# A decoder step on one core: another order of the first loads, filler transposes at the start, another order of the attention jobs

## The chip, the core and the metric

The kernel runs on one core of a Trainium2 chip. Its engines are TensorE (PE, with its weight loads as PEld), VectorE (DVE), ScalarE (ACT), GpSimd (POOL) and SyncE (SP, which here only issues DMAs). The metric is the device time of one execution in microseconds, the median of several runs.

## The reference

One inference step of a two-layer decoder with conditioning, for a prompt of 512 tokens and eight samples of 8 tokens, model width 1024, everything in float32. Cut to its shape:

```python
def trunk(x, c, ...):                       # c: one conditioning vector for each sequence
    for l in range(2):
        sh1, sc1, g1, sh2, sc2, g2 = split(silu(c) @ ada_w[l] + ada_b[l], 6)
        h = rms_norm(x, norm_g[l, 0]) * (1 + sc1) + sh1
        if l == 0:
            # h @ w_in -> xr, yg; causal depthwise conv of width 4 on xr; RG-LRU:
            #   g = sigmoid(conv(xr) @ gate_w + gate_b) -> r, i
            #   log_a = 8 r log_sigmoid(rnn_lambda);  h_t = a h_{t-1} + sqrt(1 - a^2) i x_t
            out = (rg_lru(...) * gelu(yg)) @ rnn_w_out
        else:
            out = sliding_window_attention(rope(h @ w_q), k, v, sinks) @ attn_w_o
        x = x + g1 * out
        h = rms_norm(x, norm_g[l, 1]) * (1 + sc2) + sh2
        x = x + g2 * ((silu(h @ w_gate) * (h @ w_up)) @ ffn_w_out[l])
        if l == 0:
            k, v = ...                      # own conditioning, norm, projection, rope on k
    return rms_norm(x, final_g), new states and key/value windows
```

## The kernel before

The 576 tokens stand in two halves of 288 columns (256 of the prompt, 32 of the samples), A and B. The stream x is kept transposed: 8 chunks of 128 features on the partitions, 288 columns. A weight matrix is cut into *units* of 8 tiles of 128x128. A unit is loaded into one of 4 `raw` buffers (524 KB, one DMA), then split in `convert` into a high and a low part (`wh`, 10 buffers): a cast on ScalarE and a subtract on VectorE. Activations `h` are split likewise. `product` then makes 24 matmuls of 128x288 for a unit and a half: three for each of the 8 chunks of h.

Each function below doesn't issue its instructions. `Recorder.add` records them, with the tiles that they read and write and an estimated cost, and `schedule` then plays all engines forward in time and picks for each engine the recorded instruction with the best start time, weighted with its place in the record (`prio`; `early(n)` moves a block n places ahead). The five queues run in exactly the order that `schedule` finds; the chip has no part in the choice. VectorE and GpSimd share a port in this model (`port`). SP's issues may be taken up to 60 places (SPW) out of the recorded order. Buffers are handed out with a reserve for those recorded earlier. Since every instruction is emitted in one helper, all lines of the profile are L447, and the tile names tell the instructions apart: `reg` tiles hold x before it is transposed and conditioning weights, `sl` tiles small vectors and intermediates.

The record begins with the head. c (36 KB), the samples of x and x tiles 0 and 1 are loaded on SP, then two vector loads; nine small loads go out on GpSimd's queue, among them `rnn_lambda` as eight rows of a shared tile v2. `x_half(0)` squares and transposes the first x tiles. `ada_first_load(c)` loads the columns of the first shift and scale (SH1, SC1) for chunks c and c+1, 8 DMAs of 262 KB (2.1 MB), for c = 0, 2, 4, 6, the third into `reg` buffers, of which there are five, and the others into `wh`. `ada_first(c)` multiplies them by the conditioning: 32 products of 32x128 into one PSUM tile, each of them two instructions in the trace, so 64; the four groups make 256. `ada_turn` copies the result (ScalarE) and transposes it, `ada_end` adds bias and gain (VectorE), and `modulated` makes h for these two chunks and both halves. Weight units are loaded in between (`load_more`), one before each further group. `vectors_rest` transposes v2 and the states, and `decay_rates` computes the decay's constant from `rnn_lambda` with a chain of small operations of 128x8 on VectorE; the gates of the recurrent block need it. The units come in the order x0, x1, x2, the two gate units, x3 and so on (RNN, line 52).

After the head come the recurrent block (to about 170 us), the first feed-forward block, keys and values (from about 650 us), attention (to about 810 us), the second feed-forward block and the final norm. ATT (line 53) lists the attention stage: q is a query unit (24 matmuls for a half), a an attention chunk (scores, softmax on VectorE and ScalarE, values), s a sample, f the end of a half, o an output unit; A and B are the halves.

## Time and profile before

| | us |
|---|---|
| time, median of 3 runs (1274.91 to 1280.13) | 1275.53 |
| the profiled execution | 1275.33 |
| its span | 1273.5 |
| TensorE busy | 1246.1 |
| VectorE busy | 905.7 |
| ScalarE busy | 659.4 |
| GpSimd busy | 488.2 |

The span is the time from the first instruction to the last of the profiled execution; the rest of its time lies around it. Busy time of TensorE counts from a matmul's start to its modelled end, and matmuls are pipelined: a run of instructions that overlap is all busy, however densely they follow. [...]

### The profile page before, as it was taken

What the parts mean: (1) busy time and instruction counts of PE and PEld (TensorE: products, weight loads), DVE (VectorE), ACT (ScalarE), POOL (GpSimd) and SP (SyncE); (2) the same over time, 40 slices, a digit from 0 to 9 for tenths busy, and PEclk for the clock granted to TensorE, in tenths of its full rate; (3) what the DMA queues carried; (4) which work ended last, traced back from release to release, by engine and by line L of the source; (5) the groups of instructions that cost most, each with busy time, mean ns of one, the idle gap of its engine ahead of it and who ended that gap; (6) DMA issues with size and microseconds to landing.
All of it is one profiled execution on the core that took longest, in us unless ns stands there. A gap on an engine that the chain in (4) does not pass through costs nothing.

```text
span 1273.5 us, 25461 instructions
## 1 busy us (share of the span) xinstructions
PE 1246.1 (98%) x9568; PEld 1172.8 (92%) x9568; DVE 905.7 (71%) x2156; ACT 659.4 (52%) x1469; POOL 488.2 (38%) x709
## 2 busy tenths in 40 slices
PE   7999999999999999999999999999999999999997
PEld 5798899899998998999999997999999999999997
DVE  6988885775584686467578878558857758757856
ACT  4788873762352354145357768538424425524522
POOL 3476640131551552345024436110435345335511
PEclk8999999999999999999999999999999999999999
DMA  9956554416646556444432321322333323323232
GB/s 306 315 174 199 182 166 149 157 52 211 187 141 178 180 160 199 155 150 136 125 83 56 69 76 38 111 84 96 90 94 83 100 84 96 96 78 97 71 96 75
DMA packets 223981, 165.40 MB, mean 130 GB/s; under 512 B 23757, under 2 KB 209065, under 8 KB 223826
## 3 DMA queue, kind: packets, MB, share of 16 engines
q1 hardware_dynamic: 223410, 163.45, 42.5%
q8 instruction: 75, 1.23, 0.4%
q14 instruction: 48, 0.39, 0.1%
q0 software_dynamic: 448, 0.32, 0.1%
HBM read 160.85 MB, written 4.87 MB: 130 GB/s over the span
## 4 chain that ended last, share of the span: by engine, by line
PE 73%; DVE 13%; ACT 6%; POOL 4%; issue 2%; DMA 1%; SPq 0%; ACTq 0%; POOLq 0%; DVEq 0%
PE mm L447 69%; PE ada L447 4%; DVE wh L447 4%; DVE sl L447 4%; POOL raw L447 3%; ACT wh L447 2%; DVE ta L447 1%; DMA reg<-in_x_prompt_dram 1%; DVE td L447 1%; ACT tb L447 1%; ACT h L447 1%; ACT sl L447 1%; ACT ta L447 1%; DVE tb L447 1%; DVE h L447 1%
## 5 line engine op out<-in xcount | busy, mean ns | idle before, releaser
L447 PE MATMUL mm<-h,wh 128*128 128x288 f32 x4128 | 596.8, 299 | 3.5 <-ACT h L447 2.1
L447 PEld LDWEIGHTS mm<-h,wh 128*128 128x128 f32 x4128 | 562.4, 189 | 21.7 <-issue 9.9
L447 PE MATMUL mm<-sl,wh 128*128 128x288 f32 x3218 | 462.4, 296 | 0.8 <-ACT ta L447 0.8
L447 PEld LDWEIGHTS mm<-sl,wh 128*128 128x128 f32 x3218 | 436.9, 188 | 9.4 <-issue 5.9
L447 ACT CAST wh<-raw 128x512 fp32r<-128x512 f32 (+3 forms) x388 | 266.4, 710 | 292.4 <-PE mm L447 208.4
L447 DVE TENSOR_TENSOR wh<-raw,wh 128x512 fp32r<-128x512 f32 (+3 forms) x388 | 344.9, 913 | 60.1 <-ACT wh L447 54.0
L447 POOL TENSOR_TENSOR raw<-raw 128x512 f32<-128x512 f32 x76 | 109.8, 1445 | 183.9 <-DVE wh L447 154.1
L447 POOL TENSOR_TENSOR x<-x,ta 128x32 f32<-128x32 f32 x152 | 58.7, 386 | 306.8 <-DVE ta L447 306.7
L447 DVE SCALAR_TENSOR_TENSOR x<-mm,mods,x 128x256 f32<-128x256 f32 x160 | 77.3, 483 | 133.2 <-PE mm L447 132.1
L447 POOL TENSOR_TENSOR raw<-raw,raw 128x512 f32<-128x512 f32 x76 | 111.8, 1471 | 3.7
L447 PE MATMUL mm<-tb,wh 128*128 128x288 f32 (+1 forms) x488 | 89.7, 299 | 4.5 <-POOL sl L447 1.6
L447 PEld LDWEIGHTS mm<-tb,wh 128*128 128x128 f32 x488 | 72.3, 188 | 9.4 <-DVE td L447 5.4
L447 POOL TENSOR_TENSOR td<-td,td 128x288 f32<-128x288 f32 x38 | 32.0, 843 | 111.9 <-ACT td L447 106.5
L447 ACT ACTIVATE ta<-x 128x288 f32<-128x288 f32 x56 | 24.3, 443 | 67.2 <-POOL x L447 62.1
L447 PE MATMUL mm<-ta,wh 128*128 128x288 f32 (+1 forms) x254 | 55.9, 298 | 0.0
L447 DVE TENSOR_TENSOR td<-mm,td 128x288 f32<-128x288 f32 x76 | 33.2, 452 | 27.9 <-PE mm L447 27.9
L447 PE MATMUL ada<-reg,cz 128*32 128x512 f32 (+1 forms) x448 | 49.5, 553 | 0.0
L447 DVE TENSOR_TENSOR sl<-ta,sl 128x288 fp32r<-128x288 f32 x54 | 44.9, 834 | 1.7 <-ACT sl L447 1.5
L447 ACT COPY td<-mm 128x256 f32<-128x256 f32 (+1 forms) x102 | 34.2, 353 | 20.4 <-PE mm L447 18.4
L447 DVE TENSOR_TENSOR sl<-td,sl 128x288 fp32r<-128x288 f32 x50 | 38.2, 764 | 8.1 <-ACT sl L447 8.1
L447 ACT ACTIVATE ta<-mm 128x288 f32<-128x288 f32 x54 | 21.4, 410 | 43.2 <-PE mm L447 41.8
L447 PEld LDWEIGHTS mm<-ta,wh 128*128 128x128 f32 x254 | 41.5, 188 | 1.8 <-ACT wh L447 0.8
(202 smaller groups left out, 1248.4 us busy)
## 6 DMA issues: line engine op xcount, KB each, us to landing
raw<-in_ffn_w_in_dram SPq DMA_DIRECT2D x88, 512.0 KB
reg<-in_ada_w_dram SPq DMA_DIRECT2D x80, 512.0 KB
raw<-in_ffn_w_out_dram SPq DMA_DIRECT2D x32, 384.0 KB
raw<-in_ffn_w_out_dram SPq DMA_DIRECT2D x32, 320.0 KB
raw<-in_rnn_w_in_dram SPq DMA_DIRECT2D x16, 512.0 KB
reg<-in_kv_ada_w_dram SPq DMA_DIRECT2D x16, 512.0 KB
wh<-in_ada_w_dram SPq DMA_DIRECT2D x24, 256.0 KB
raw<-in_rnn_w_out_dram SPq DMA_DIRECT2D x8, 512.0 KB
```

Source lines behind the costliest of these rows:

```text
L447: self.rec.add(eng, lambda: getattr(obj, name)(*map(real, args), **{k: real(v) for k, v in kw.items()}), cost, outs, ins, func, lat, port, ...
```

## The change

The start of the record is written anew. `rnn_lambda` gets a load and a tile of its own, the first load on GpSimd's queue; `decay_rates` transposes it itself and stands near the start of the record, 200 places later in priority (DK). SP's loads up to weight unit 2 are recorded in one piece and issued in exactly that order (`strict`). `keep_busy(200)` records 200 transposes of the identity into a PSUM tile that nothing reads; `schedule` takes one on PE only where its next other instruction would start more than 250 ns (FILL) later, and drops those left over once all up to `idle_end` is done. `ada_first` puts its products into the queue in batches of 8 (first group) or 16 (the others), which nothing can come between, and its transpose goes to the conditioning's own PSUM pool. The order of attention jobs is another, the model's rule for the shared port is another, and conditioning products are planned at n/2.4 + 6 instead of n/2.4 + 30 ns. The arithmetic of the outputs stays the same.

```diff
-ATT = ("q0A q2A a0A q1A q0B a2A a1A q1B q3A a0B q2B a1B q4A a3A a4A q3B a2B q5A q4B a3B q6A a5A q5B q7A a6A a4B s0A "
-       "q6B a5B s1A s2A s3A q7B a7A s0B a6B fA s2B a7B s1B o0A s3B o1A fB o2A")
+ATT = "q0A q2A a0A q1A q0B a2A q1B q3A a0B q2B q4A a1A a1B a4A a3A q3B a2B q5A q4B a3B q6A a5A q5B q7A a6A a4B s0A q6B a5B s1A s2A s3A q7B a7A s0B fA s2B a6B a7B s1B o0A s3B o1A o2A fB"
...
+FILL = 250
+DK = 200
+AF_ = (1, 2, 2, 2)
...
                 for pr, i, op in avail[e]:
-                    if e == "SP" and i > sp_next + SPW:
+                    if op.idle:
+                        fill = fill or op
+                        continue
+                    if e == "SP" and i > sp_next + (SPW if i >= self.strict else 0):
                         break
...
                     if op.port == 1:
-                        s = max(s, port - 130 if e == "DVE" else port + 20)
+                        s = max(s, port - 100 + (60 if holder == e else 0))
...
+                if fill and fill.prio <= limit:
+                    at = alloc_time(fill, f)
+                    if at is not None:
+                        s = max(f, fill.ready, at)
+                        if pick is None or pick[1] > s + FILL:
+                            pick = (0, s, fill, False)
...
-                cost = n / 2.4 + 30 if dt == F32 else n / 9.6 + 15
+                cost = n / 2.4 + 6
...
+    lam_ = sl()
+    lam = lam_.f[0:8, 0:P]
+    G.dma_start(lam, a["rnn_lambda"][0].rearrange("(r p) -> r p", p=P))
...
     def decay_rates():
...
+        pt = aux()
+        T.transpose(pt[:, 0:8], lam, ident[0:8, 0:8])
+        V.tensor_copy(lamT, pt[:, 0:8])
...
-    def ada_first(c):
+    def ada_first(c, m):
         o = ps(pada, "ada")
-        for q, b in enumerate(first_w[c]):
-            for k in range(2):
-                ada_mm(o, 2 * q + k, [b.f[:, n : n + P] for n in (256 * k, 256 * k + P, 512 + 256 * k, 512 + 256 * k + P)], q + k == 0, q + k == 4)
-            b.done()
-        t = ada_turn(o, 1)[:, 0:P].rearrange("p (g c b) -> p g c b", g=2, c=2)
+        for q0 in range(0, 4, m):
+            with rec.together():
+                for q in range(q0, q0 + m):
+                    b = first_w[c][q]
+                    for k in range(2):
+                        ada_mm(o, 2 * q + k, [b.f[:, n : n + P] for n in (256 * k, 256 * k + P, 512 + 256 * k, 512 + 256 * k + P)], q + k == 0, q + k == 4)
+                    b.done()
+        t = ada_turn(o, 1, ps(pada, "ada"))[:, 0:P].rearrange("p (g c b) -> p g c b", g=2, c=2)
...
-    x_half(0)
-    ada_first_load(0, whs)
-    vectors()
-    load_more(1)
+    def keep_busy(n):
+        with rec.when_idle():
+            t = aux()
+            for i in range(n):
+                T.transpose(t[:, 0:P], ident[:], ident[:])
+
+
+    keep_busy(200)
+    with early(-DK):
+        decay_rates()
+    load_more(nload[0] - nconv[0] + 1)
     for t in (2, 3):
         x_load(t)
+    ada_first_load(0, whs)
+    convert()
+    load_more(nload[0] - nconv[0] + 1)
+    ada_first_load(2, whs)
+    ada_first_load(4, regs)
+    convert()
+    ada_first_load(6, whs)
+    load_more(nload[0] - nconv[0] + 1)
+    convert()
+    rec.strict = len(rec.ops)
+    x_half(0)
+    vectors()
     H[0], H[1] = hkind[0](F32R), hkind[1](F32R)
     for c in range(0, KC, 2):
-        if c < 6:
-            convert()
-        ada_first(c)
-        if c < 6:
-            load_more(ST[c // 2])
-            ada_first_load(c + 2, (whs, regs, whs)[c // 2])
+        ada_first(c, AF_[c // 2])
...
     vectors_rest()
+    rec.idle_end()
...
-    with early(100):
-        decay_rates()
```

## Rows read from the trace of the kernel before

**Rows 1.** The page's busy time, share of the span and instructions of each engine

```profile
PE 1246.1 (98%) x9568; PEld 1172.8 (92%) x9568; DVE 905.7 (71%) x2156; ACT 659.4 (52%) x1469; POOL 488.2 (38%) x709
```

**Rows 2.** Stretches: us, busy (instructions) of PE, PEld, DVE, ACT, POOL, PEclk, DMA, GB/s

```profile
0.00:53.10 53.10, 43.03 (x414) 31.32 (x414) 39.65 (x179) 28.85 (x64) 15.81 (x37) 0.90 1.05 320
...
53.10:150.00 96.90, 96.87 (x724) 86.78 (x725) 83.43 (x162) 85.29 (x170) 66.00 (x143) 1.00 0.58 187
...
150.00:170.00 20.00, 17.10 (x126) 14.94 (x125) 14.79 (x27) 15.09 (x27) 11.34 (x27) 1.00 0.55 178
...
690.00:700.00 10.00, 8.32 (x63) 7.83 (x62) 9.06 (x22) 8.34 (x21) 6.23 (x6) 1.00 0.25 55
```

**Rows 3.** The head in stretches of 10 us, columns as above

```profile
0.00:10.00 10.00, 4.96 (x32) 4.83 (x33) 1.75 (x8) 5.15 (x8) 6.12 (x20) 1.00 0.76 232
10.00:20.00 10.00, 6.61 (x83) 3.77 (x81) 8.77 (x37) 3.76 (x9) 2.50 (x6) 0.99 1.11 339
20.00:30.00 10.00, 9.74 (x60) 6.70 (x60) 8.50 (x32) 5.77 (x13) 2.46 (x5) 0.50 1.11 345
30.00:40.00 10.00, 8.83 (x119) 6.01 (x118) 8.82 (x41) 5.07 (x13) 3.08 (x4) 1.00 1.14 328
40.00:50.00 10.00, 9.98 (x104) 7.48 (x105) 9.15 (x54) 6.00 (x15) 1.65 (x2) 1.00 1.11 344
```

**Rows 4.** The chain that ended last: start us, length us, what

```profile
12.63 8.10 DMA reg<-in_x_prompt_dram
...
250.09 49.77 PE mm L447 x372
```

**Rows 5.** TensorE in order of time: start us, length us, what, count

```profile
7.09 1.75 PE L447 MATMUL mm<-ident,reg 128*128 128x128 f32 x7
...
9.49 0.72 PE L447 MATMUL mm<-ident,reg 128*128 128x128 f32 x5
...
20.87 1.94 PE L447 MATMUL mm<-ident,reg 128*128 128x128 f32 x8
...
33.55 0.65 PE L447 MATMUL ada<-reg,cz 128*32 128x128 f32 x16
...
38.88 0.63 PE L447 MATMUL ada<-reg,cz 128*32 128x128 f32 x12
...
42.90 0.40 PE L447 MATMUL mm<-h,wh 128*128 128x288 f32 x1
...
47.15 0.63 PE L447 MATMUL ada<-wh,cz 128*32 128x128 f32 x12
...
48.24 4.67 PE L447 MATMUL mm<-h,wh 128*128 128x288 f32 x32
```

**Rows 6.** Groups of TensorE up to 53.1 us: what, count, busy us, mean ns

```profile
L447 PE MATMUL mm<-h,wh 128*128 128x288 f32 x94 | 19.9, 341 | 1.4 <-ACT h L447 1.4
...
L447 PE MATMUL ada<-wh,cz 128*32 128x128 f32 x192 | 11.6, 307 | 0.9 <-DVE cz L447 0.4
...
L447 PE MATMUL ada<-reg,cz 128*32 128x128 f32 x64 | 3.4, 279 | 0.0
...
L447 PE MATMUL mm<-ident,reg 128*128 128x128 f32 x32 | 6.1, 362 | 1.9 <-DVE tb L447 1.7
```

**Rows 7.** SyncE's issues in order of time, columns as in rows 5

```profile
4.13 5.77 SPq L447 DMA_DIRECT2D wh<-in_ada_w_dram  x8
```

**Rows 8.** The chain that ended last, around 690 us

```profile
690.95 2.86 DVE wh L447 x2
...
695.03 1.05 ACT wh L447
```

**Rows 9.** Groups of VectorE from 14 to 51.3 us, columns as in rows 6

```profile
L447 DVE TENSOR_SCALAR sl<-sl 128x8 f32<-128x8 f32 x35 | 5.8, 165 | 0.3
...
L447 DVE SCALAR_TENSOR_TENSOR sl<-sl 128x8 f32<-128x8 f32 x27 | 4.8, 182 | 0.5
...
L447 DVE TENSOR_TENSOR sl<-sl 128x8 f32<-128x8 f32 x18 | 3.5, 195 | 0.4
```

More of the change, by code (lines that the diff above doesn't have):

```diff
@@ L85 @@
 class Op:
-    __slots__ = ("i", "prio", "eng", "emit", "cost", "func", "preds", "succ", "npred", "ready", "allocs", "start", "end", "done", "lat", "tiles", "port", "mode")
+    __slots__ = ("i", "prio", "eng", "emit", "cost", "func", "preds", "succ", "npred", "ready", "allocs", "start", "end", "done", "lat", "tiles", "port", "mode", "idle")
 class Ref:
@@ L139, in __init__ @@
         self.batch = None
+        self.fills = []
+        self.strict = 0
     @contextmanager
@@ L152, in together, with when_idle, idle_end @@
         self.add(b[0][0], emit, sum(x[2] for x in b), [y for x in b for y in x[3]], [y for x in b for y in x[4]], mode=self.mode)
+    @contextmanager
+    def when_idle(self):
+        self.fills.append([len(self.ops), None, True])
+        yield
+        self.fills[-1][1:] = len(self.ops), False
+    def idle_end(self):
+        self.fills[-1].append(len(self.ops))
     def tile(self, pool, kind, cap, reserve, shape, dt, name):
@@ L183, in add @@
         op.eng, op.emit, op.cost, op.func, op.lat = eng, emit, cost, func, lat
-        op.port, op.mode = port, mode
+        op.port, op.mode, op.idle = port, mode, bool(self.fills) and self.fills[-1][2]
         op.preds, op.succ, op.allocs, op.tiles = set(), [], [], set()
@@ L232, in schedule @@
         cold = 0.0
-        port, mode = 0.0, 0
+        port, holder, mode = 0.0, "", 0
         pos = {n: j for k in self.order for j, n in enumerate(self.order[k])}
@@ L274, in schedule @@
         sp = deque(o.i for o in self.ops if o.eng == "SP")
-        rest = deque(sorted(self.ops, key=lambda o: o.prio))
+        rest = deque(sorted((o for o in self.ops if not o.idle), key=lambda o: o.prio))
         done = set()
+        fills = deque(self.fills)
         while n_left:
             best = None
+            while fills and (not rest or rest[0].prio >= fills[0][3]):
+                for op in self.ops[fills[0][0] : fills[0][1]]:
+                    if op.i in done:
+                        continue
+                    done.add(op.i)
+                    n_left -= 1
+                    if op.npred == 0:
+                        avail["PE"].remove((op.prio, op.i, op))
+                    for n in op.tiles & last.keys():
+                        last[n] -= 1
+                        if last[n] == 0:
+                            if n in got:
+                                slots[self.kind_of[n]].append(rel_at[n] + 260)
+                            got.add(n)
+                fills.popleft()
+            if not n_left:
+                break
             while sp and sp[0] in done:
@@ L288, in schedule @@
                 seen = 0
+                fill = None
                 for pr, i, op in avail[e]:
-                    if e == "SP" and i > sp_next + SPW:
+                    if op.idle:
+                        fill = fill or op
+                        continue
+                    if e == "SP" and i > sp_next + (SPW if i >= self.strict else 0):
                         break
@@ L332, in schedule @@
             if op.port == 1:
-                port = s + cost
+                port, holder = s + cost, e
             elif op.port == 2 and s + 60 < port:
@@ L627, in vectors_rest @@
         pt = aux()
-        T.transpose(pt[:, 0:88], v2[0:88, :], ident[0:88, 0:88])
-        V.tensor_copy(abT[:, 96:112], pt[:, 72:88])
-        V.tensor_copy(vecT[:, 32:104], pt[:, 0:72])
+        T.transpose(pt[:, 0:80], v2[0:80, :], ident[0:80, 0:80])
+        V.tensor_copy(abT[:, 96:112], pt[:, 64:80])
+        V.tensor_copy(vecT[:, 32:96], pt[:, 0:64])
+        V.tensor_scalar(hgb[:], vecT[:, 80:96], 0.5, None, ALU.mult)
         pt = aux()
@@ L646, in decay_rates @@
         z, neg, msk, scl, p_, w_, w2, s_ = [tw.f[:, 8 * i : 8 * i + 8] for i in range(8)]
-        V.tensor_scalar(hgb[:], vecT[:, 80:96], 0.5, None, ALU.mult)
+        pt = aux()
+        T.transpose(pt[:, 0:8], lam, ident[0:8, 0:8])
+        V.tensor_copy(lamT, pt[:, 0:8])
+        lam_.done()
         V.tensor_scalar(neg, lamT, -1.0, None, ALU.mult)
@@ L691, in ada_mm, with ada_turn @@
             T.matmul(o[32 * j : 32 * j + 32, 0 : _free(w)], cz[:, k, :], w, start=first, stop=last)
-    def ada_turn(o, n):
-        t = aux()
+    def ada_turn(o, n, t):
         for i in range(0, n, 2):
@@ L764, in ada_step @@
             if k == KC - 1:
[L765 removed]
+                t = ada_turn(o, 4, aux()).rearrange("p (q g c b) -> p g c q b", q=4, g=2, c=2)
                 for i, g in enumerate(pairs[u // 16]):
```

4 lines of the change are left out of this document (1 added, 3 removed).

## The prediction, made before the changed kernel ran

> **What bounds the kernel now.** I read the busy times of the page first. TensorE is busy 98% of the span [rows 1], so only three things can shorten the kernel: less idle time on TensorE, less time at its low clock, and a denser queue. Then I cut the span into stages. From 53.1 to 150 us TensorE is idle for 0.03 us; up to 53.1 us it is idle for 10.1 us and the granted clock averages 0.90; 150 to 170 us loses 2.9 us and 690 to 700 us loses 1.7 us [rows 2]. The head is thus the place to look, and the diff works mostly there.
>
> In slices of 10 us the head shows its limit: from 10 us on the DMA engines are busy all the time and move 328 to 345 GB/s, while TensorE sits at the low clock from 20 to 30 us and VectorE is busy for 8.5 to 9.15 of every 10 us [rows 3]. Busy is not the same as useful, so I weigh the work. A long run of 128x288 products takes 49.77/372 = 0.134 us each [rows 4]. Sixteen conditioning products take 0.65 us, one alone lasts 0.279, so they follow each other after (0.65-0.28)/15 = 0.025 us; five transposes at 9.49 us take 0.72, so with a last one of the same length (0.72-0.28)/4 = 0.11 us each [rows 5, 6]. Up to 53.1 us the queue holds 94 products, 256 conditioning products and 64 transposes, of which the 32 of the prompt are the largest group [rows 6]: 94 x 0.134 + 256 x 0.025 + 64 x 0.11 = 12.6 + 6.4 + 7.0 = 26.0 us of work. So the head loses 27 us. After it the queue is dense: 32 products in 4.67 us [rows 5].
>
> **The change, part by part.** *The loads.* I count bytes in the order of the queue. The rows of GB/s add up to 2.3 MB at 10 us, 5.7 at 20, 9.2 at 30 and 12.4 at 40 [rows 3]. The last x tile stands at 5.3 MB in the old order (about 18.7 us) and its transfer is over at 12.63 + 8.10 = 20.7 us [rows 4], so a load is usable some 2 us after its bytes have had their turn. The old order puts the last conditioning load at 13.1 MB, behind one rnn_gate unit: turn at 42, usable at 44 us. The new order puts weight unit 0 and x tiles 2 and 3 ahead of the conditioning and lets nothing but unit 1 in between: the four groups of 2.1 MB end at 5.3, 7.9, 10.0 and 12.1 MB, usable at 20.7, 28.3, 34.5 and 40.9 us, and unit 2 at 12.6 MB, 42.5 us. The first group comes 4.5 us later than before, the last 3 us earlier. On SP the same issues are made in another order, eight of them in 5.77 us [rows 7] for bytes that need 6.2, so SP stays ahead; but the strict order means that a load whose buffer isn't free holds all behind it. The buffers in question are the five of x and conditioning (free once x is transposed, by about 20 us) and the weight buffers, free as the first two groups are consumed (by 30 us), each earlier than the turn of the load that waits for it. If one were late, it would cost its lateness, up to 2 us.
>
> *What TensorE can do with them.* From the last conditioning product of a group (38.88 + 0.63) to a 128x288 product on its output (42.90) it took 3.4 us [rows 5]; I use 4. So by the new landings: group by group 0.4 to 1 us of conditioning, then, 4 us later, 24 products on units 0 and 1 (3.2 us) for each pair of chunks; TensorE waits for data through all of it. The gate is at the end: unit 2 lands at 42.5, its cast on ScalarE takes 1.05 and its subtract on VectorE 2.86/2 = 1.4 [rows 8], with about 1 us of queueing: 46 us. By then six chunks of units 0 and 1 are done (72 products), the last two chunks come from 45 to 48, and from 46 on there is work without a break: 36 products on unit 2, 36 on the last chunks. The useful work at 46 us is 72 x 0.134 + 6.4 + 7.0 = 23.0 us, a loss of 23.0 us against 27.1 before: **4.1 us gained**. Bounds: 7 us if unit 2 doesn't gate (the last products of a group then end at 42 with the loss at some 20), 1 us if VectorE is as late as before (the old head's last conditioning products end at 47.15 + 0.63 = 47.8, 3.8 us behind the landing at 44 [rows 5]).
>
> *The decay rates.* Their three large groups are 80 operations on VectorE, 14.1 us in all, spread over 14 to 51 us [rows 9], a stretch in which it is 85 to 92% busy [rows 3]. Their own load lets them start near 7 us, where VectorE is nearly idle (1.75 of the first 10 us). By the share of the time, 14.1 x 21/37 = 8 us of VectorE's work leave the stretch from 30 to 51 us. It isn't a gain of its own; it is why I let the new head follow its landings more closely. The first conditioning in batches of 8 and 16 products does the same for TensorE's queue: in the old head a single 128x288 product stands between two groups of conditioning, as at 42.90, and lasts 0.40 us [rows 5] where one in a run costs 0.134. I cost both at nothing beside the 4.1.
>
> *The fillers.* Up to 200 transposes of the identity where the planner sees TensorE idle for over 0.25 us. They carry no work; they can raise the clock and they can stand in the way. [...] The fillers start near 1.6 us, once the identity is built; if they ran at the low level as long as the old head's transposes did, until about 6 us, they would take 0.21 instead of the 0.107 planned there, 2 us of lag. The planned idle up to 46 us is 46 - 23 - 2 = 21 us, less some 40 gaps under 0.25 us that stay: 100 to 150 fillers, not all 200. Since each gap leaves slack, the lag is gone by 20 us, when the first group lands. Cost 0, bounds 0 to 3 us. The clock from 20 to 30 us is full then, which in a stretch that waits for data is part of the 4.1.
>
> [...]
>
> *The attention order.* At 690 to 700 us TensorE is idle for 1.7 us while VectorE is busy for 9.06 of 10; the chain runs through two weight subtracts of VectorE (2.86 us) and a cast (1.05) [rows 2, 8]. The new order puts three query products ahead of two attention chunks, whose softmax steps are VectorE and ScalarE work, so the conversions come earlier. I take 1.0 of the 1.7; bounds -1.5 (the same stall at another place) and 1.7.
>
> *The planner's costs.* Port rule and cost of conditioning products change orders only. No row shows what another order is worth; the nearest, the 2.9 us of 150 to 170 us, bounds it to 2 us either way. I take 0.
>
> The sum goes against the profiled execution, 1275.33 us (span 1273.5 and 1.8 around it), which is 0.2 below the median of the three: 1275.3 - 4.1 - 1.0 = 1270.2, or 1270.4 on the median. I forecast **1270.3 us**.
>
> **The rivals.** *Faster still.* VectorE free of the decay rates converts unit 2 at once, TensorE is dense from 44 us (6 us gained), the stall at 690 us goes wholly (1.7) and the one at 150 us partly (1): 1275.3 - 8.7 = 1266.6. For it: the lag of 3.8 us behind the landing. Against: unit 2 is last in the queue. *Given back.* The recurrent stage after the head keeps ScalarE busy for 85 and VectorE for 83 of 97 us [rows 2]; if they set its pace, the 4 us come back as idle time at 150 to 170 us: 1274.5. Against: TensorE is idle for 0.03 us there. *Fillers in the way, slower or level.* If all 200 go out, the point at which 26 us of work are done lies at 1.6 + 2 + 200 x 0.11 + 26 + 4 (gaps) = 55.6 us against 53.1: 2.5 us lost, 1277. It decides from about 175 fillers. *Slower: the fillers don't raise the clock.* 130 of them then take 0.1 us more each, 13 us, and the work among them is slow too; a few microseconds of that are hidden in waits for data, so 8 to 12 us reach the end: 1284. [...] *The fillers or the loads don't go where they should* (the planner's data times are wrong, and TensorE waits at the low clock as before): the loads alone then give 2 to 3 us, 1273.
>
> **How the numbers follow.** Forecast 0.38; faster still 0.29; given back or misplaced (1273 to 1274.5) 0.20; fillers in the way 0.09; clock not raised 0.04. About 0.5% (6.4 us) is what a measurement of this kernel can tell from no change: faster means under 1269.2, slower over 1281.9. The rival below that and a third of the forecast's band (1267 to 1273) make faster 0.42; slower is the last rival and a little of the one before, 0.05; the rest, 0.53, is within. The range reaches from 1264.5 (head 7, attention 1.7, other orders 2) to 1277.
>
> **What would show it.** Right: the x tiles ahead of the conditioning on SP, the last conditioning products by 43 us, fillers from under 2 us, a granted clock of 1.00 from 10 us on, decay operations over by 25 us, and about 32 more products of 128x288 done at 53 us (126 instead of 94). Wrong: conditioning products that end after 46 us, unit 2 converted after 48, more than 175 fillers, a low clock after 10 us, or new idle time at 150 to 170 us.

## The result, and the profile after

The changed kernel takes **1262.64 us** (median of 4 runs, 1261.47 to 1262.99) against 1276.53 of the kernel before, run beside it: a ratio of 0.989 (0.987 to 0.992). Forecast were 1270.3 us, with 1264.5 as the lower end. So the time fell by 13.9 us where 5 were forecast, and lies 1.9 us below the range. The profiled execution's span is 1261.1 us against 1273.5, that is 12.4 less.

The page's busy time after the change, to be held against [rows 1]:

```profile
PE 1246.3 (99%) x9704; PEld 1182.5 (94%) x9704; DVE 883.6 (70%) x2157; ACT 650.3 (52%) x1464; POOL 494.2 (39%) x709
```

TensorE is busy for as long as before, and yet 12 us are gone. VectorE does one instruction more and is busy for 22 us less. That is the first sign that something other than the head changed. The four stretches of [rows 2], after (us, busy time and instructions of PE, PEld, DVE, ACT, POOL, PEclk (the granted clock of TensorE as a share of full speed), DMA share, GB/s):

```profile
0.00:53.10 53.10, 50.34 (x561) 44.15 (x562) 38.48 (x183) 29.33 (x67) 16.54 (x40) 1.00 1.03 312
53.10:150.00 96.90, 96.83 (x728) 86.79 (x727) 83.72 (x154) 79.02 (x161) 67.77 (x139) 1.00 0.60 192
150.00:170.00 20.00, 19.96 (x149) 19.68 (x148) 19.03 (x36) 17.32 (x34) 12.20 (x23) 1.00 0.51 170
690.00:700.00 10.00, 10.00 (x77) 10.00 (x76) 7.97 (x23) 2.89 (x6) 6.36 (x12) 1.00 0.72 133
```

The idle time of 150 to 170 us and of 690 to 700 us is gone. The head is now filled (with transposes) at a granted clock of 1.00; how much useful work it does is told by the count of 128x288 products up to 53.1 us, 105 instead of 94:

```profile
L489 PE MATMUL mm<-ident 128*128 128x128 f32 x135 | 20.1, 300 | 1.4 <-POOL tst L572 1.4
...
L489 PE MATMUL mm<-h,wh 128*128 128x288 f32 x105 | 17.3, 309 | 0.3 <-POOL h L489 0.3
```

**Where the time went.** All kernels here run the same 8088 products of 128x288 (96 of them are of 128x300; numbered in order of time), so the start of product n is a clock that runs on useful work. The table gives, for one profiled execution of each kernel, how much longer (+) or shorter (-) each stage is than in the kernel before, in us. Products 0 to 400 are the head, to 1000 the rest of the recurrent block, to 3700 the first feed-forward block, to 4200 its end and keys and values (591 to 666 us before), to 4600 the first queries (to 741), to 5000 the attention (to 838), to 8087 the second feed-forward block. The last column is the mean, in ns, of the 54 subtracts `sl<-ta,sl`, of which more below. Two executions of one kernel (after, after_beside) differ by up to 1.5 us in a stage.

| kernel | time, ratio to before | to 400 | 1000 | 3700 | 4200 | 4600 | 5000 | 8087 | sum | ns |
|---|---|---|---|---|---|---|---|---|---|---|
| before, length of the stage | 1276.5 | 100.5 | 92.8 | 398.2 | 74.7 | 74.5 | 97.7 | 426.1 | | 834 |
| after | 1262.6, 0.989 | -1.2 | -2.9 | -0.5 | -3.4 | -3.3 | +2.2 | -3.4 | -12.5 | 502 |
| after_beside | 1261.9, 0.989 | -2.3 | -2.9 | -0.5 | -3.1 | -1.8 | +2.2 | -4.3 | -12.7 | 501 |
| port_only | 1268.5, 0.995 | -0.5 | -2.3 | +0.8 | -3.7 | -2.4 | +4.9 | -4.1 | -7.3 | 490 |
| port_att | 1266.8, 0.993 | +5.2 | -1.2 | -0.8 | -3.4 | -2.8 | +2.4 | -3.5 | -4.1 | 493 |
| head_only | 1271.5, 0.997 | -0.7 | -2.5 | -0.1 | -0.2 | +0.8 | +0.2 | -0.7 | -3.2 | 854 |
| att_undone | 1266.1, 0.991 | -0.9 | -2.9 | -0.5 | -3.4 | -2.4 | +4.9 | -4.1 | -9.4 | 501 |
| pool_half | 1279.5, 1.002 | -0.8 | -2.2 | +0.6 | -2.9 | -0.4 | +13.9 | -3.9 | +4.3 | 493 |
| placebo1 | 1283.8, 1.006 | +3.7 | -1.9 | -0.5 | -1.0 | +0.6 | +6.4 | -1.2 | +6.2 | 922 |
| after_beta | 1265.5, 0.992 | -1.6 | -3.4 | -0.9 | -3.6 | -4.7 | +7.7 | -3.6 | -10.0 | 491 |

The sum after is -12.5 us, and the head is the smaller part of it in these executions. Columns 4200 and 8087 separate by the port rule: -2.9 to -4.3 in the seven executions that have it or half of it, -0.2 to -1.2 in the two that don't.

### The profile page after: what moved, and what is told of

It is laid out like the page before. It is cut to its first block, busy times and chain, and to the rows that moved or that the text cites. A ratio compares the mean times of both kernels' runs of the same rounds, so it can differ in the third digit from the quotient of the medians.

```text
span 1261.1 us, 25732 instructions
## 1 busy us (share of the span) xinstructions
PE 1246.3 (99%) x9704; PEld 1182.5 (94%) x9704; DVE 883.6 (70%) x2157; ACT 650.3 (52%) x1464; POOL 494.2 (39%) x709
## 4 chain that ended last, share of the span: by engine, by line
PE 88%; ACT 5%; DVE 3%; DMA 2%; POOL 1%; issue 1%; SPq 0%; ACTq 0%; DVEq 0%
PE mm L489 84%; PE ada L489 4%; DMA wh<-in_ada_w_dram 1%; ACT h L489 1%; ACT ta L489 1%; ACT tb L489 1%; DVE sl L489 1%; ACT sl L489 1%; DVE ta L489 1%; DMA raw<-in_rnn_w_in_dram 1%; DVE wh L489 1%; ACT wh L489 1%; SPq L489 0%; ACT td L489 0%; ACT L489 0%
## 5 line engine op out<-in xcount | busy, mean ns | idle before, releaser
L489 DVE TENSOR_TENSOR wh<-raw,wh 128x512 fp32r<-128x512 f32 (+3 forms) x388 | 340.5, 900 | 63.9 <-ACT wh L489 59.6
L489 ACT COPY td<-mm 128x256 f32<-128x256 f32 (+1 forms) x102 | 33.5, 357 | 13.9 <-PE mm L489 13.9
L489 ACT CAST sl<-ta 128x288 fp32r<-128x288 f32 x54 | 23.4, 433 | 31.8 <-DVE ta L489 29.4
L489 ACT ACTIVATE ta<-ta,stat 128x256 f32<-128x256 f32 (+2 forms) x72 | 32.5, 474 | 9.6 <-DVE stat L489 9.3
```

Of the source, the lines that this page charges most:

```text
L489: self.rec.add(eng, lambda: getattr(obj, name)(*map(real, args), **{k: real(v) for k, v in kw.items()}), cost, outs, ins, func, lat, port, ...
```

## The experiments

### The parts apart

port_only is the kernel before with the new port rule alone. In this rule `port` is the time at which the planner expects the port of its model, the one that it lets VectorE and GpSimd share, to be free, and `holder` the engine that took it last. The old rule lets VectorE start up to 130 ns before that time and GpSimd no sooner than 20 ns behind it; the new one lets either start 100 ns before it, or 40 if it is the holder itself. port_att has the new attention order and the new cost of conditioning products besides; head_only is the changed kernel with these three undone; no_fillers is the changed kernel without its transposes of the identity.

```diff
-        port, mode = 0.0, 0
+        port, holder, mode = 0.0, "", 0
...
-                        s = max(s, port - 130 if e == "DVE" else port + 20)
+                        s = max(s, port - 100 + (60 if holder == e else 0))
...
-                port = s + cost
+                port, holder = s + cost, e
```

> The kernel before with the planner's new rule for the port that VectorE and GpSimd share, and nothing else. Theory 1: the gain outside the head (11 of 12.4 us by the progress of the 128x288 products) comes from this rule, whose orders keep the two engines off each other: busy time of VectorE falls by about 15 to 22 us and the time by 7 to 9, to 1267 to 1269 us. Theory 2: the gain outside the head is a consequence of the new head (all that follows starts from another state): 1274 to 1277 us, VectorE's busy time as before. Theory 3: any change of the orders moves the time by several us, and this rule is no better than another: anywhere from 1268 to 1283.

> The kernel before with the new port rule, the new attention order and the new cost of conditioning products; the head's record is the old one. Theory 1: 1263.5 to 1266 us, all of the gain but the 1.1 us by which the new head is ahead at 100 us. Theory 2: 1272 to 1276. Theory 3: 1264 to 1280.

> The changed kernel with the old port rule, the old attention order and the old cost of conditioning products: only the head's record is new (loads, batches, decay rates, fillers). Theory 1: the head's 1 to 2 us alone, 1274 to 1276 us. Theory 2: most of the gain, 1264 to 1268. Theory 3: 1266 to 1280, with the head 1 to 2 us ahead at 100 us and the rest scattered.

```diff
-    keep_busy(200)
...
-    rec.idle_end()
```

> The changed kernel without the filler transposes. [...] If the head waits for its loads whatever the clock: 1262 to 1263, and the 20 us of busy time that they show cost nothing and bring nothing.

Measured: port_only 1268.46 (0.995, 0.993 to 0.997), port_att 1266.75 (0.993, 0.991 to 0.996), head_only 1271.50 (0.997, 0.995 to 0.998), no_fillers 1261.56 (0.989, 0.986 to 0.991). The kernel before, beside these four, took 1276.16. The rule that I costed at nothing brings most, 7.7 us; the head that I costed at 4.1 brings 4.7 by head_only, and the fillers bring nothing. (The profiled execution of port_att is the longest of its five, 1271.25, and loses its 5 us in the old head.)

### What the rule changes in the feed-forward blocks

In the second feed-forward block TensorE is busy all the time before and after, but the same 200 us hold 18 more instructions after. Before and after:

```profile
960.00:1160.00 200.00, 199.38 (x1495) 197.78 (x1494) 142.21 (x244) 84.48 (x165) 88.55 (x86) 1.00 0.31 88
```

```profile
960.00:1160.00 200.00, 200.00 (x1513) 200.00 (x1512) 135.61 (x249) 85.81 (x168) 90.74 (x88) 1.00 0.32 91
```

The second busy time, of TensorE's weight loads, shows the gaps (197.78 of 200) that the pipelined matmuls cover; the busy time of PE hides them. The starts of the matmuls show them too: between products 6000 and 8000 (978 to 1250 us before) 41 of them start 0.08 to 0.46 us later than the 0.134 us of a dense run, 5.5 us in sum; after, 19 do, 1.6 us in sum. One group of VectorE stands out (838 us to the end; count, busy us, mean ns), before and after:

```profile
L447 DVE TENSOR_TENSOR sl<-ta,sl 128x288 fp32r<-128x288 f32 x19 | 21.0, 1104 | 0.5 <-ACT sl L447 0.5
```

```profile
L489 DVE TENSOR_TENSOR sl<-ta,sl 128x288 fp32r<-128x288 f32 x19 | 8.5, 450 | 0.0
```

Same instruction, 2.5 times as long. The order of time around one of them, before:

```profile
970.36 3.28 POOL L447 TENSOR_TENSOR raw<-raw,raw 128x512 f32<-128x512 f32 x2
...
972.41 1.55 DVE L447 TENSOR_TENSOR sl<-ta,sl 128x288 fp32r<-128x288 f32 x1
...
973.88 0.45 DVE L447 TENSOR_TENSOR mm<-mm,ta 128x288 f32<-128x288 f32 x1
...
979.08 0.45 DVE L447 TENSOR_TENSOR td<-mm,td 128x288 f32<-128x288 f32 x1
...
979.58 0.43 PEld L447 LDWEIGHTS mm<-tb,wh 128*128 128x128 f32 x3 [0.21 <-DVE td L447]
```

and after:

```profile
961.78 3.28 POOL L489 TENSOR_TENSOR raw<-raw,raw 128x512 f32<-128x512 f32 x2
...
964.70 0.47 DVE L489 TENSOR_TENSOR mm<-mm,ta 128x288 f32<-128x288 f32 x1 [0.79 <-PE mm L489]
965.07 0.45 DVE L489 TENSOR_TENSOR sl<-ta,sl 128x288 fp32r<-128x288 f32 x1
```

Before, the subtract (low part of an activation, nothing is in a hurry for it) runs beside a GpSimd instruction, lasts 1.55 us instead of 0.45, and stands ahead of the add into PSUM (`mm<-mm,ta`). From it on VectorE has no pause until `td<-mm,td`, the use of a PSUM bank for which TensorE's next products wait (979.58). After, the add comes first, and the subtract starts when the GpSimd pair is over (965.06). Before, the pair ends at 973.64 and the subtract 0.32 us behind it, at 973.96. Twelve of the 19 subtracts of this block start while a GpSimd instruction runs, and all twelve end 0.31 to 0.32 us behind it: eleven last 1.54 to 1.55 us, beside `raw<-raw,raw`, and one 0.83, beside `td<-td,td`; the other seven last 0.45. The add, which has one operand in PSUM, lasts 0.47 us beside GpSimd (964.70, after). What makes the subtract end so late, the traces don't show; that all twelve do is what the argument needs.

To see whether this order is the cause, swapped takes the kernel before and moves such a subtract behind the add on VectorE's queue, all other queues as they were (`rec.subs` and `rec.adds` mark these two instructions where they are recorded); swapped_ffn2 does so in the second block alone.

```diff
     order_ = rec.schedule()
+    dve = [o for o in order_ if o.eng == "DVE"]
+    for j, p in enumerate(dve[:-2]):
+        for q in dve[j + 1 : j + 3]:
+            if p.i in rec.subs and q.i in rec.adds:
+                order_.remove(p)
+                order_.insert(order_.index(q) + 1, p)
```

> The kernel before, all queues as they were, but for one thing on VectorE: in the feed-forward blocks, where the low-part subtract of a gate product (sl<-ta,sl) stands one or two places ahead of the add into a PSUM bank on which TensorE goes on accumulating (mm<-mm,ta), it is put right behind that add. Theory 1 (what the new port rule buys in the feed-forward blocks is this order: the subtract meets a GpSimd operation and lasts 1.55 us instead of 0.45, and the add and with it TensorE wait behind it): the second feed-forward block (860 to 1265 us) gets 3 to 4.5 us shorter, the time falls to 1271.5 to 1273.5. Theory 2 (the stretched subtracts cost TensorE nothing; the gain lies in another change of the order): 1275 to 1277, no stage shorter by over 1 us.

> The kernel before with VectorE's queue alone altered, in the second feed-forward block alone: where a subtract into sl (the low part of an activation) stands one or two places ahead of an add into PSUM, it is moved right behind that add. All other queues are identical, and the first 800 us are the old ones. Theory (the stretched subtract ahead of the PSUM add costs TensorE some 0.3 us each, inside its busy time): the second block is 3.5 to 5 us shorter, 1271.5 to 1273.0 against 1276.5, the mean of the sl<-ta,sl subtracts of this block falls from about 0.8 us toward 0.5, and TensorE's weight loads are busy for 19.9 to 20.0 of 20 us there. Rival (what the new rule gains is not this order but the order as a whole, and TensorE would lose the same time at another place of the block): within 1.5 us of the kernel before.

swapped: 1274.72 (0.999, 0.997 to 1.000). By the count of products its second block is 5.1 us shorter than before, where after's is 3.4, but it loses 3.1 us between products 3700 and 4200:

```profile
600.00:610.00 10.00, 8.06 (x52) 5.54 (x51) 8.33 (x11) 3.95 (x8) 4.48 (x4) 0.83 0.01 2
```

```profile
605.12 1.06 PE L448 MATMUL mm<-tb,wh 128*128 128x288 f32 x6 [1.94 <-DVE td L448]
```

TensorE waits 1.94 us for VectorE and the granted clock averages 0.83 in these 10 us. swapped_ffn2, without that place: **1272.18 (0.997, 0.996 to 0.998)**, 2.8 us less in the second block, at most 0.4 elsewhere, the group's mean 536 ns. It gives 3.5 us by the medians (1275.72 beside it) and 3.8 by its trace; its theory asked 3.5 to 5 of the block alone, which gave less.

One edit thus shows 5.1 and 2.8 us in one block. Counted finer, both kernels gain 2.9 us between products 6000 and 8000, where the stretched subtracts stand, and the late starts fall from 41 to 25 (2.5 us in sum). The executions with the rule or half of it gain 3.4 to 4.0 there; head_only and placebo1, without it, change by +0.2 and -0.1. The other differences of this column lie before product 6000, where two executions of the changed kernel differ by 0.9 too. So the place of this subtract is shown to be worth about 3 us in the second block, which is most of what the rule gains there; the rest was not separated.

The length of the subtract costs nothing by itself. In the first block its mean falls from 875 ns to 455 in swapped and 448 in port_only, and that block is 0.2 and 0.8 us longer, not shorter. What counts is whether something that TensorE waits for stands behind it.

### Which half of the rule

pool_half changes only what the rule says of GpSimd:

```diff
-                        s = max(s, port - 130 if e == "DVE" else port + 20)
+                        s = max(s, port - 130 if e == "DVE" else port - 100)
```

> The kernel before with half of the new port rule: an operation of GpSimd may be planned 100 ns before the other engine leaves the port instead of 20 ns after it; VectorE's side stays at 130 ns before. Theory (what counts is where the low-part subtracts stand, which comes from what the rule says of a VectorE operation that follows another VectorE operation; GpSimd's side alone gives no gain but another order): the mean of sl<-ta,sl stays between 0.7 and 0.9 us, and the time is 1272 to 1284 as for an arbitrary new order. Rival (GpSimd's earlier starts bring the gain): the mean falls to 0.5 us and the time to 1267 to 1270.

1279.46 (1.002, 1.001 to 1.004). The time is one that my theory gave, but its reason is wrong: the subtracts fell to 493 ns, and the stages to 4200 and to 8087 gain as with the whole rule. Letting GpSimd be planned closer to VectorE is enough for these gains. The time is 0.2% longer all the same, since this order loses 13.9 us in the attention, where one wait of TensorE for a ScalarE result reaches 1.9 us and the granted clock averages 0.66 from 800 to 810 us. What the other half of the rule is worth alone was not tried.

### Keys and values, 655 to 670 us

This stage gains 3.4 us in after, 3.7 by the new rule alone, and 0.2 to 1.0 without it (head_only, placebo1). TensorE's products on the new h and GpSimd's share of h, before (start, length, count, wait):

```profile
661.71 0.96 PE L447 MATMUL mm<-h,wh 128*128 128x288 f32 x6
...
663.48 0.53 PE L447 MATMUL mm<-h,wh 128*128 128x288 f32 x2 [0.81 <-ACT wh L447]
...
664.77 4.12 PE L447 MATMUL mm<-h,wh 128*128 128x288 f32 x16 [0.76 <-ACT h L447]
...
665.46 1.92 POOL L447 TENSOR_TENSOR h<-tb,h 128x256 fp32r<-128x256 f32 x2
```

and after:

```profile
652.26 0.75 POOL L489 TENSOR_TENSOR h<-tb,h 128x256 fp32r<-128x256 f32 x1 [0.41 <-ACT h L489]
...
656.53 3.99 PE L489 MATMUL mm<-h,wh 128*128 128x288 f32 x26
...
661.26 0.66 PE L489 MATMUL mm<-h,wh 128*128 128x288 f32 x3 [0.74 <-ACT wh L489]
```

The stretch 660 to 670 us before, after, in after_beside and in swapped_ffn2:

```profile
660.00:670.00 10.00, 8.43 (x51) 7.61 (x50) 9.24 (x21) 10.00 (x23) 3.75 (x5) 0.83 0.27 57
```

```profile
660.00:670.00 10.00, 9.26 (x69) 8.64 (x68) 9.31 (x25) 6.18 (x12) 7.49 (x6) 1.00 0.58 107
```

```profile
660.00:670.00 10.00, 9.60 (x60) 9.22 (x61) 7.78 (x21) 4.74 (x10) 6.69 (x6) 0.83 0.55 107
```

```profile
660.00:670.00 10.00, 8.02 (x57) 7.04 (x56) 9.41 (x23) 10.00 (x22) 4.11 (x6) 1.00 0.28 60
```

Before, two waits (0.81 and 0.76 us) come close together, and one of 0.49 us stands at 604 us; after, one of 0.74 is left, and it falls behind product 4200, into the next stage. These three waits, with the late starts behind the second, come to 3.1 us by the starts of the matmuls, nearly the whole gain of this stage. The clock is not its cause. It averages 0.83 before and 1.00 after, but after_beside, the same kernel as after, has 0.83 too and keeps the gain (-3.1); and swapped_ffn2, which has the order of before here and both its waits, has 1.00 and gains nothing (0.0). What the fall of the clock costs shows in the next stage, 1.5 us: -1.8 in after_beside where after has -3.3. After, GpSimd takes its share of h earlier (652 us; before from 665.46 on). This is read from the traces and agrees with the seven executions of the table; no run tested it alone.

### How much is the order as such

placebo1 changes one of the planner's weights in the kernel before, after_beta the same in the changed one. It means nothing in itself and gives another order from about 60 us on.

```diff
-BETA = 0.75
+BETA = 0.74
```

> The kernel before with the weight of an instruction's place in the planner's choice (BETA) at 0.74 instead of 0.75: another order without a reason for it. If any new order moves this kernel by several us (theory 3), 1268 to 1283, with stages that gain and lose 2 to 4 us; VectorE's busy time stays near 905. If the port rule's gain is its own, 1274 to 1278.

> The changed kernel with the planner's weight of the recorded order at 0.74 instead of 0.75, which means nothing in itself and gives another order from 60 us on. In the kernel before the same edit cost 7.2 us. Theory (the new rule puts the subtracts in the right place in any order, but 3 to 7 us of the gain belong to this one order): the mean of sl<-ta,sl stays at 0.45 to 0.55 us and the time is 1263 to 1270. Rival (the gain is the rule's alone): 1261 to 1263.5. Rival (it is luck of the order altogether): 1270 or more, the subtracts stretched again.

placebo1: 1283.76 (1.006, 1.004 to 1.008). after_beta: 1265.49 (0.992, 0.990 to 0.994). An arbitrary new order cost 7 us before and 3 after, most of it in the attention (+6.4; +7.7 against +2.2). With the rule the subtracts stay short in either order (491 ns); without it they don't (922). So the gains at 4200 and 8087 belong to the rule, and some 3 us, mostly of the attention, to this one order.

### The attention order

att_undone is the changed kernel with the old order of the attention jobs.

> The changed kernel with the old order of the attention jobs. By the progress of the products the new port rule alone loses about 4 us in the attention stage, which the kernel with both doesn't. Theory 1 (the new attention order fits the new rule): 1265.5 to 1267 us. Theory 2 (the loss came from the state in which that stage began): 1262 to 1263.5. My prediction's step, a stall of 1 us at 690 us: 1263.5.

1266.14 (0.991, 0.989 to 0.994): the new order is worth 3.5 us by the medians, about as much as after_beta's meaningless edit moves this kernel. The stages show it twice: the attention loses 4.9 us with the old order (port_only, att_undone) and 2.2 to 2.4 with the new (after, port_att). The new order under the old rule was not tried.

### The head

The forecast had TensorE dense from 46 us on. In the trace after it is dense from 49.00, and the order of time shows what came late:

```profile
42.57 1.49 POOL L489 TENSOR_TENSOR h<-tb,h 128x256 fp32r<-128x256 f32 x1 [4.12 <-ACT h L489]
...
44.12 0.93 PE L489 MATMUL mm<-h,wh 128*128 128x288 f32 x5 [0.27 <-POOL h L489]
...
44.98 1.08 PE L489 MATMUL ada<-wh,cz 128*32 128x128 f32 x32
...
46.13 0.27 ACT L489 COPY ta<-ada 128x128 f32<-128x128 f32 x1 [1.89 <-PE ada L489]
46.29 1.05 ACT L489 CAST wh<-raw 128x1024 fp32r<-128x1024 f32 x1
...
47.72 1.23 DVE L489 TENSOR_TENSOR wh<-raw,wh 128x1024 fp32r<-128x1024 f32 x1
...
49.00 6.26 PE L489 MATMUL mm<-h,wh 128*128 128x288 f32 x45
```

The last conditioning batch stands in TensorE's queue behind products that wait for GpSimd; ScalarE waits 1.89 us for its result, and the cast of unit 2 stands behind that copy. Three suspects, three edits: the decay rates (dk_early records them 400 places earlier instead of 200 later; they are then over by 22.6 us instead of 41.6), unit 2 (unit2_first loads it ahead of the last conditioning group), and the place of the last batch (batch_ahead2 moves it right behind the one before, and its copy and transpose with it; p and q are the two batches of the last group). batch_unit2_2 makes the last two edits together.

```diff
-DK = 200
+DK = -400
```

> The changed kernel with the decay rates 400 places ahead in priority instead of 200 behind. In the changed kernel 60 of some 85 of their operations still ran between 20 and 40 us, where VectorE is busy for 9.2 of 10 us, and the head did 105 products by 53.1 us where 126 were predicted. If that is why: the decay rates end before 25 us, 112 to 126 products by 53.1 us, and the time falls by 1 to 3 us, to 1259.5 to 1261.5. If the head waits for something else (the order of TensorE's queue, GpSimd), 105 +- 4 products and 1262 to 1263.

```diff
-    ada_first_load(6, whs)
     load_more(nload[0] - nconv[0] + 1)
+    ada_first_load(6, whs)
```

> The changed kernel with one load moved: SyncE issues weight unit 2 ahead of the last conditioning group (chunks 6 and 7) instead of behind it. Theory (in the new head unit 2's conversion, over at 49.0 us, is the gate, and what held it is that ScalarE's cast of it stands behind a wait for the last conditioning copy): unit 2 lands near 36 us, its products begin well before 46, at least 112 products of 128x288 are done at 53.1 us instead of 105, and the time falls by 1 to 3 us against the changed kernel, to 1259.5 to 1261.5. Rival (the gate is the last two chunks, so the last conditioning group, which now lands 1.6 us later): 100 to 106 products at 53.1 us and a time of 1262.5 to 1264.5.

```diff
     order_ = rec.schedule()
+    p, q = rec.last
+    order_.remove(q)
+    order_.insert(order_.index(p) + 1, q)
+    t = next(o for o in rec.ops[q.i + 1 :] if o.eng == "PE")
+    pe = [o for o in order_ if o.eng == "PE"]
+    order_.remove(t)
+    order_.insert(order_.index(pe[pe.index(q) + 9]) + 1, t)
+    u = next(o for o in rec.ops[q.i + 1 :] if o.eng == "ACT")
+    if order_.index(u) > order_.index(t):
+        order_.remove(u)
+        order_.insert(order_.index(t), u)
```

> As batch_ahead, in which the transpose of the result did not wait for ScalarE's copy and so turned values that were not there yet; here the copy stands ahead of it (two places earlier on ScalarE's queue), so nothing of the computation is left out. The last 32 conditioning instructions stand right behind the first half, the transpose behind seven products. Theory: the copy of the result, at 46.13 us before the edit, comes at 43.4 to 44.5, unit 2's subtract, over at 48.95, is over by 47.2, 115 to 122 products are done at 53.1 us instead of 105, and the time falls by 1 to 2 us, to 1260.6 to 1261.6. Rival (the last load lands later than I computed, or VectorE is the bound of this stretch): the products at 53.1 stay at 103 to 108 and the time at 1262 to 1264.

> As batch_unit2, with ScalarE's copy ahead of the transpose, so that nothing is left out: unit 2 is loaded ahead of the last conditioning group, and the last batch, which ran at 46.85 us, stands right behind the first half (over at 44.5). Theory: the copy of the result comes at 45.5 to 46.2 instead of 47.99, 110 to 120 products at 53.1 us instead of 99, time 1259.5 to 1261. Rival (the load, which is now last and lands 1.6 us later, sets the time): the batch runs at 45.5 or later, under 106 products at 53.1 us, time 1261.5 to 1263.

dk_early: 1263.65 (0.989), 93 products at 53.1 us; unit2_first: 1261.89 (0.989), 99 products. Neither decay rates nor unit 2 alone held the head. In unit2_first unit 2 is converted at 41.8, but the last batch then runs at 46.85. batch_ahead2: 1258.87 (0.988), 121 products, and the lowest time of all; batch_unit2_2: 1261.54 (0.988), 105 products, its copy at 45.18, as the theory had it, but VectorE converts another unit (46.43, 1.23 us) ahead of the conditioning. (In a first form of these two, batch_ahead and batch_unit2, the transpose didn't wait for the copy and turned values that were not there yet; their 1260.97 and 1260.45 us are not read here.)

batch_ahead2 is 3.8 us under the changed kernel, but didn't run beside it, so both kernels ran once more side by side:

> The changed kernel itself, on the same chip and in the same rounds as the next run. Theory (the place of the last conditioning batch costs 2 us of the head, and they reach the end): 1261.5 to 1263. Rival (the difference to the next kernel is one between chips): both kernels within 0.7 us of each other.

> The same kernel as batch_ahead2, nothing left out. Theory: 1.5 to 3 us under the changed kernel beside it, 1259 to 1260.5, with some 121 products of 128x288 done at 53.1 us. Rival: within 0.7 us of it; then the 16 products more at 53.1 us are given back later.

after_beside 1261.89 (1260.58 to 1263.10), batch_ahead3 1261.49 (1260.72 to 1262.26): the rival's 0.7 us hold, and no difference is measured at the end. batch_ahead3 is the kernel of batch_ahead2, on the same chip, and its median is 2.6 us higher; so differences of this size between kernels that did not run side by side need more than their medians. batch_ahead3, from its last group on:

```profile
41.27 1.95 PE L490 MATMUL ada<-wh,cz 128*32 128x128 f32 x64
43.59 0.24 ACT L490 COPY ta<-ada 128x128 f32<-128x128 f32 x1
44.35 1.05 ACT L490 CAST wh<-raw 128x1024 fp32r<-128x1024 f32 x1
45.88 1.23 DVE L490 TENSOR_TENSOR wh<-raw,wh 128x1024 fp32r<-128x1024 f32 x1
```

Both batches run without a break from 41.27 on, so the load was there by 42.3, as computed; the copy comes 2.5 us and unit 2's subtract 1.8 us earlier than in after. And yet this execution has 114 products at 53.1 us, and the one of batch_ahead2, the same kernel, has 121; the changed kernel has 105 in one and 113 in the other. The start accounts for it. The 32 fillers at the beginning, and the first instruction behind them, which VectorE waits for; after, and after_beside:

```profile
1.44 6.20 PE L489 MATMUL mm<-ident 128*128 128x128 f32 x32 [1.44 <-POOL tst L572]
7.57 0.22 PE L489 MATMUL mm<-ident,sl 8*128 8x8 f32 x1
```

```profile
1.44 5.06 PE L489 MATMUL mm<-ident 128*128 128x128 f32 x32 [1.44 <-POOL tst L572]
6.43 0.22 PE L489 MATMUL mm<-ident,sl 8*128 8x8 f32 x1
```

The same 32 transposes take 5.06 us in one execution and 6.20 in another, by the moment at which they get faster: in the stretch 4.4 to 5.4 us 12 of them run, in whole or in part, in after_beside and 7 in after. The first conditioning batch comes 11.07 us later in both (17.50, 18.65), and so in batch_ahead2 (6.75 to 17.82) and batch_ahead3 (7.64 to 18.71). Without fillers that first instruction runs at 5.52 us.

## Why the prediction was wrong, point by point

**The planner's costs: forecast 0 with bounds of 2 us, measured 7.7** (port_only, 1268.46 against 1276.16 beside it; 7.3 by the traces). This is the step that failed. I wrote that no row shows what another order is worth, and bounded it by one stall. Two figures of the trace before did show that there was something to gain: PEld at 197.78 of 200 us in a stretch where PE is full, and a group of VectorE whose mean was 834 ns when its shortest took 450. I had read only stages with idle time of TensorE, and the feed-forward blocks have next to none. By its trace the rule alone gives -3.7 (keys and values), -2.4 (queries), -4.1 (second block), -2.3 (recurrent block, where head_only and placebo1 gain 2.5 and 1.9 without it) and +4.9 (attention). In the second block its mechanism is shown by swapped_ffn2 for about 3 us; in keys and values it is read; for the queries no cause was found; in the attention it is a loss that goes with the order and differs from kernel to kernel by up to 11.7 us (2.2 to 13.9). The rival "faster still" (1266.6) is the nearest in number, but not for its reasons: unit 2 was not converted at once, and TensorE is dense from 49 us, not from 44.

**The head: forecast -4.1, measured -1.2 and -2.3** at product 400 in two executions, with 105 and 113 products at 53.1 us where 126 were forecast, but 4 to 5 us by the medians: head_only lies 4.7 us under the kernel before beside it, and after 4.1 under port_att, from which it differs in the head alone (not run side by side). One pair of traces doesn't show this, since the old head varies from execution to execution. In port_att it is 5.2 us longer than in the profiled execution of before, with a granted clock of 0.50 from 20 to 30 us and of 0.84 from 30 to 40, where before has 0.50 and 1.00; and beside port_only the kernel before took 1273.3 us at a mean granted clock of 0.997 and 1278.6 at 0.992, while ten executions of head_only stay within 1270.0 to 1273.8. What makes the old head vary was not tested; the low clock alone is not enough, since no_fillers has it too (0.50 from 20 to 30 us) and loses nothing. So the size agrees with the medians, but not by the path that I computed. Loads and landings were right: from 10 to 40 us the DMA engines move 340 to 344 GB/s (328 to 345 before, [rows 3]), and the clock is up:

```profile
20.00:30.00 10.00, 9.80 (x136) 7.84 (x135) 9.30 (x53) 4.55 (x11) 3.20 (x7) 1.00 1.10 344
30.00:40.00 10.00, 9.95 (x145) 8.53 (x145) 9.21 (x50) 5.13 (x14) 1.50 (x2) 1.00 1.11 342
```

Two steps of the working fell. "The lag is gone by 20 us": it isn't, since VectorE's queue starts with the instruction behind the fillers, and is busy for 9.1 to 9.3 of 10 us from 10 to 40 us; the lag of 0.9 to 2.1 us (6.43 or 7.57 against 5.52) is still there at product 400. And "the last two chunks come from 45 to 48": the batch that they need ran at 44.98 instead of 43. batch_ahead3 takes 9 products (114 against 105, 1.2 us) out of its place. For the executions with and without this edit, gain, lag and place add up alike: after 1.2 + 2.05 + 1.2 = 4.4, after_beside 2.3 + 0.9 + 1.2 = 4.4, batch_ahead2 3.3 + 1.2 = 4.5, batch_ahead3 2.4 + 2.1 = 4.5. So against this one execution of before the new order of loads would give about 4.4 without these two, an account that no single run shows. That the 1.2 us of the place reach the end isn't shown either (0.4 us between the medians).

**The fillers: cost 0, right, for a half-wrong reason.** 135 up to 53.1 us (100 to 150 forecast); without them 1261.56. They cost the lag, and what they give back is the clock, which without them is 0.50 from 20 to 30 us, with them 1.00:

```profile
20.00:30.00 10.00, 7.99 (x77) 5.30 (x78) 8.55 (x30) 5.30 (x13) 3.95 (x9) 0.50 1.11 345
```

I held both to be hidden; that they cancel is read from these numbers, not tested apart. TensorE does get faster while it runs nothing but transposes: in after the fillers follow each other after 0.213 us up to 6.40 us and after 0.109 from 6.61 us on; in after_beside 5 or 6 of them ran, in whole or in part, in each microsecond up to 3.4 us, and 11 or 12 from 4.4 us on. So it does in the old head: seven transposes at 7.09 us take 1.75 us, five at 9.49 take 0.72 [rows 5]. The granted clock reads 1.00 in all these stretches, so that it is the clock which rises there is my inference; what the trace shows of the clock itself is the 1.00 against 0.50 from 20 to 30 us. The 0.21 us a filler from which I worked out the lag held; that it is gone by 20 us did not. The rival by which the fillers don't raise the clock is out, and so are fillers in the way.

**The attention order: forecast -1.0, measured -3.5** (1266.14 against 1262.64), at another place. The stall at 690 us goes with the port rule alone (port_only: TensorE busy for 10.00 of 10 us there); the new order gains in the attention itself, 740 to 838 us, which I hadn't considered. That the sign was right is luck: the reason I gave is not what the runs show. The medians of the parts (rule 7.7, head 4.1 to 4.7, attention order 3.5) add up to more than the 13.9 measured; so they overlap, or carry the scatter of runs that were not made side by side.

**The decay rates.** Forecast over by 25 us; they ended at 41.6, since they stand 200 places later in priority. I let them pay for the head's closeness to its landings; dk_early shows that ending them by 22.6 us brings nothing.

**The recurrent stage, 150 to 170 us,** gains 2.9 us, where the rival "given back" saw a loss and "faster still" a gain of 1. Every kernel with another order has 1.2 to 3.4 of it, head_only and placebo1 too, and swapped and swapped_ffn2, which keep the old order there, have 0.0 and -0.1; so that stall belonged to the one order of the kernel before.

## What to carry to other kernels

Where an engine's busy time is full, look at how much it gets done: the weight loads beside the matmuls (here 197.78 of 200 us), instructions in equal stretches (1495 against 1513 in 200 us), and groups of which the mean is far above the shortest (1104 and 446 ns). A long instruction is worth only what waits behind it: in the first block the subtracts fell from 875 to 448 ns for no gain. A rule that only reorders is to be costed by such rows, by every stage, and not by the idle time of the bound engine; an arbitrary reordering of this kernel moves it by 3 to 7 us, which is as much as most of its edits. The work put in front of this queue as filler delayed what stood behind it by 0.9 to 2.1 us, and VectorE, busy for 9.1 to 9.3 of 10 us from then on, carried the delay along to product 400.

## What was not expected of the hardware

- A VectorE subtract of 128x288 lasts 0.45 us alone and 1.55 us beside GpSimd's `raw<-raw,raw` of 128x512; 11 of the 19 in the second feed-forward block did so before, one more took 0.83 us beside `td<-td,td`, and after all 19 take 0.45 (21.0 and 8.5 us in all).
- The granted clock can fall behind waits of less than a microsecond, in some executions of a kernel and not in others: behind one wait of 0.75 us and twelve products of a single column it averages 0.83 over 10 us in after_beside and 1.00 in after. The 100 products from product 4200 on take 18.9 us with the fall and 17.4 without. Behind waits of 0.81 and 0.76 us it falls in before and not in swapped_ffn2, and 16 products then take 4.12 and 3.32 us.
- The moment at which TensorE gets faster after its start differs from execution to execution of one kernel by over 1 us (32 transposes in 5.06 us in after_beside and 6.20 in after), and the head moves with it: the first conditioning batch comes 11.07 us behind the instruction after them in both.
